# One function table for Ln and Exp, written table loads, and a chunk-by-chunk opening in a hybrid decoder layer

## The chip, the cores and the metric

The kernel runs on one core of one Trainium2 chip. The metric is the time of one execution on the device, in microseconds; of several runs the median is given. TensorE (PE in the rows), VectorE (DVE), ScalarE (ACT) and GpSimd (POOL) are the core's engines, SyncE (SP) issues most of the transfers.

## The reference, cut to what matters

One decoder layer over 512 tokens of width 1024, in float32:

```python
x = x + 0.5 * swiglu(rms_norm(x, ffn1_norm), ffn1_w_gate, ffn1_w_up, ffn1_w_down)
x = x + hybrid_mixer(rms_norm(x, mix_norm), ...)
x = x + 0.5 * swiglu(rms_norm(x, ffn2_norm), ffn2_w_gate, ffn2_w_up, ffn2_w_down)
return rms_norm(x, final_norm)
```

`swiglu` has a hidden width of 2816. `hybrid_mixer` projects once (`w_in`) and runs two branches on the result: a dilated sliding-window attention (12 heads of 64 in three groups, whose outputs are merged by their softmax denominators), and RWKV-7 time mixing (16 heads of 64):

```python
kk = kk / jnp.maximum(jnp.sqrt(jnp.sum(kk * kk, axis=-1, keepdims=True)), 1e-12)
# per token t and head: S_t = S_{t-1} diag(w_t) + (S_{t-1} a_t) b_t^T + v_t k_t^T ;  y_t = S_t r_t
g = jax.nn.sigmoid(zg) @ g2
yn = (y - mu) * lax.rsqrt(var + RWKV_GN_EPS)          # group norm of each head
merged = gates[:, :D] * y_attn + gates[:, D:] * y_rwkv # then one output projection
```

`zg` has 160 columns: 128 of them make one full projection of the kernel, the other 32 a small one.

## The kernel before, in words

**Layout and products.** Everything lies transposed: features on the 128 partitions, 512 tokens in the free dimension, so a matrix of activations is 8 chunks of 128x512. A float32 product is made of three matmuls in fp32r, `mm3` (L383): high part of the weight times high part of the activation (`xhi`), high times low (`xlo`), low times high. A weight of 128x1024 is 8 blocks, so 24 matmuls of 128x128 by 512 columns, called full matmuls here.

**Weights.** `wload` (L448) issues a weight's transfer on SyncE's queue into one of three raw buffers `wr`; `wsplit` (L459) copies it to `wh` on ScalarE and subtracts to `wl` on VectorE. There are two pairs of `wh` and `wl`, so the split of a weight waits for the last matmul of the one before the last. `wnext` and `wahead` call them, the latter after the third block of a weight.

**The start (from L501).** ScalarE loads the table that holds Sqrt. X comes in 8 chunks on SyncE's queue, the first weight in two halves between them; `vec`, the small vectors (the norm's gains among them), comes on GpSimd's queue. For each chunk `gain_chunk` makes `xhi` (ScalarE) and `xlo` (VectorE), and `sum_chunk` squares the chunk (ScalarE, `t` or `ssq`) and adds (VectorE). Then the feed-forward, `ffn`, goes weight by weight: the 24 matmuls of the first gate weight into one accumulator `facc`, the 24 of the first up weight into another, and after them `norm_rstd` (a matmul of the sum of squares by a constant, Sqrt, reciprocal). Since the scale 1/rms is applied behind the product, the matmuls needn't wait for it.

**The mixer.** Its calls are not issued as they are written but recorded as nodes of a `Plan`; `Plan.order` (L217) is a list scheduler that walks all engines with a cost for each node (`note`, from L131), a penalty for a change of the array's tile mode, and rules on buffers, and `emit` (L349) issues the nodes in that order. The projections are main work, in the order of the table `MAIN_ORDER`; beside them run streams of side work: `post` (for each of 8 head pairs: decay, norm of k, masks), `finish` (for four groups of two such pairs, called a pair here: inversion of the chunk's triangular matrices, then the recurrence over 8 chunks of 64 tokens with the state in `SVU`), `tail` (group norm, bonus and output gate of a pair) and `core` (two of attention). All matmuls of the side work are small, in float32.

**Tables.** Sigmoid and Tanh, Exp, Ln, Sqrt and Silu are table functions of ScalarE. The kernel before leaves the loads of the mixer to the compiler, which puts an `ACT_TABLE_LOAD` in front of a function whose table isn't the one loaded. `rsqrt` (L755), called in `post` and `tail` for each of the 8 head pairs, computes 1/sqrt as Exp(-0.5 Ln s) with a Newton step: Ln, Exp and Square on ScalarE, two operations on VectorE.

**The places of the change.** `rsqrt` and `tail` (L1123): the scale of the group norm's variance is a `tensor_scalar` on VectorE. `h_zg2` (L800) and the loop over `MAIN` (L1271): the small gate projection is `mm3` over 8 blocks of 32 columns, 24 matmuls. Lines 358 and 377 in the rows are helpers: L358 is the call in `emit`, so all that the plan issues, L377 the call of a `Queue` outside it, so both feed-forwards.

Of the kernel before, what the change touches and what calls it, by code (L numbers as in the profile page):

```python
# [17 lines left out]
P = 128  # L18
# [29 lines left out]
MAIN_ORDER = """  # L48
k.0 r.0 v.0 k.1 r.1 v.1 gate.0 gate.1 gate.2 gate.3 k.2 gate.4 r.2 v.2 r.3 k.3 v.3 gate.5 gate.6 gate.7 gate.8 k.4 r.4
v.4 k.5 r.5 gate.9 v.5 gate.10 gate.11 gate.12 gate.13 gate.14 gate.15 k.6 r.6 v.6 k.7 r.7 v.7 aq.0.0 av.0.0 aq.0.1  # L50
ak.0.1 av.0.1 aq.0.2 ak.0.0 av.0.2 ak.0.2 av.1.2 av.1.0 aq.1.0 aq.1.1 ak.1.0 ak.1.1 av.1.1 aq.1.2 ak.1.2 wout.0 wout.1
wout.2 wout.3 wout.4 wout.5 wout.6 aup.0 wout.7 aup.1"""
# [3 lines left out]
LAT, SLACK, WINDOW, HOLD, SETTLE = 0.07, 0.2, 40, 0.0, 3.5  # L56
URGENT, SIDE, MAIN_MM = range(3)


# [26 lines left out]
class Plan:  # L86


    TABLES = {"Sigmoid": "sigmoid", "Tanh": "sigmoid", "Exp": "exp", "Ln": "exp", "Sqrt": "sqrt", "Silu": "silu"}

    def __init__(self):
# [39 lines left out]
    def note(self, eng, op, call, outs, ins, func=None):  # L131
        tags = [k[0] for k in map(self.slot, outs + ins) if k]
        if eng == PE:
# [3 lines left out]
            c = n / 2400 + 0.0136 if x.dtype == F32R else 4 * n / 2400 + 0.01  # L137
            c = 0.018 if mode == (32, 32) else c * 0.5 if 64 in mode else c
            nd = self.open
# [77 lines left out]
    def order(self, keep):  # L217
# [19 lines left out]
        for nd in self.nodes:  # L237
            for tag in {k[0] for k in uses[nd]}:
                touch.setdefault(tag, []).append((nd, [k for k in nd.new if k[0] == tag], [k for k in uses[nd] if k[0] == tag and k in mortal]))

        def safe(nd):

            for tag in {k[0] for k in nd.new}:
                bufs = next(k[1] for k in nd.new if k[0] == tag)
                u = used.get(tag, 0) + sum(k[0] == tag for k in nd.new)
                if u > bufs:
                    return False
                rest = {}
                l = touch[tag] = [x for x in touch[tag] if x[0] not in done]
                for m, new, ends in l:  # L250
                    if m is not nd:
                        u += len(new)
                        if u > bufs:
                            return False
                    for k in ends:
                        n = rest[k] = rest.get(k, left[k]) - 1
                        if not n:
                            u -= 1
            return True

        while len(done) < len(self.nodes):
# [29 lines left out]
            elif eng == PE:  # L291
                if nd.mode[0] != mode:
                    c += 0.2 if nd.mode[0] == (128, 128) else 0.1
                mode = nd.mode[1]
                free[PE] = t + c
                end = t + c + 0.17
            else:
                if nd.table and nd.table != table:
                    c += 1.3
                    table = nd.table  # L300
                if nd.lock:
                    t = max(t, port)
                    port = t + c
                end = free[eng] = t + c
# [7 lines left out]
            for k in nd.new:  # L312
# [3 lines left out]
                self.place[k[2]] = f[1]  # L316
            for k in uses[nd]:
                left[k] -= 1
                if not left[k] and k in mortal:
# [29 lines left out]
    def emit(self, tc, keep):  # L349
        self.on = False  # L350
        with tc.manual_schedule():
            for nd in self.order(keep):
                for tag, _, name in nd.new:
                    if tag in self.rings:
# [37 lines left out]
def layer_kernel(ctx: ExitStack, tc, a, out):  # L392
# [110 lines left out]
    vec = const.tile([P, NVEC], F32, name="vec")  # L503
    G.dma_start(vec, a["vec"])
    cst = const.tile([P, CST["bd"]], F32, name="cst")
# [4 lines left out]
    A.preload_act_table_set("sqrt_and_others")  # L510
    xload(0)
    wload(2, lambda i: xload(1 + i))
    xload(3)
    wload()
    for m in range(4, DC):
        xload(m)
    Y.dma_start(cst, a["cst"][:, 0:CST["bd"]])
    wsplit(2)
    omka = const.tile([P, 8], F32, name="omka")
# [52 lines left out]
    def ffn(tag, X, hpool, tmp, rstd_fn, done, stack):  # L572
# [7 lines left out]
        for f in range(FC):  # L580
            pg, pu = facc(), facc()
            for part, ps in ((0, pg), (1, pu)):
                w = wnext((tag, "gu", f, part))
# [40 lines left out]
    def tmp():  # L624
        return hpool.tile([P, S], F32, tag="tmp", bufs=5, name=nm("t"))
    for m in range(DC):
        gain_chunk(X[:, m, :], col("ffn1_norm", m), m)
    wsplit()
    for m in range(DC):
        sum_chunk(ssq, X[:, m, :], m, tmp)  # L630
    ssq1 = acts.tile([P, S], F32, tag="ssqa", bufs=1, name=nm("ssq"))
# [60 lines left out]
def mixer(tc, a, env):  # L692
# [17 lines left out]
    with ExitStack() as st:  # L710
# [89 lines left out]
        def h_zg2(ps):  # L800
            z = shift_evac(ps, 2, 32)
            A.activation(z[0:32, 0:S], z[0:32, 0:S], AF.Sigmoid)
# [320 lines left out]
        def tail(q, Qt, YT, raws):  # L1123
            for hl in range(2):
# [7 lines left out]
                rs = b2()  # L1132
                V.tensor_scalar(rs[:, 0:S], ps, 1.0 / 64.0, GN_EPS, op0=ALU.mult, op1=ALU.add)
                rs = rsqrt(rs)
# [134 lines left out]
        rstd = None  # L1269
        wz = lora_w(lora_load(a["w_zg2"]))  # L1270
        for t in MAIN:  # L1271
            n = t[0]
            w = wnext(t)
            if n in handlers:
# [8 lines left out]
                if n == "zg":  # L1283
                    ps = acc()
                    plan.stream = "main"
                    for k in range(DC):
                        plan.cls = MAIN_MM
                        mm3(T, ps[0:32, :], wsl((wz[:, 0:256], wz[:, 256:512]), k, 32), xk(k), k == 0, k == DC - 1)
                        plan.cls = SIDE
# [157 lines left out]
```

## Time and profile before

| | |
|---|---|
| median of 3 runs | 1404.8 us (1403.41 to 1405.29) |
| the profiled execution | 1407.91 us, its span 1406.1 us |
| mean granted clock of TensorE | 0.99 |
| busy, of the span | TensorE 97%, VectorE 59%, ScalarE 43%, GpSimd 1% |
| transfers | 158.5 MB, mean 113 GB/s |

The stages by the timeline: first feed-forward to 374 us, projections with RWKV and then attention to 1032, with the output projections behind, second feed-forward and final norm to the end. A row of the trace's groups gives the operation, its output and inputs by name (`b` is any of the mixer's 128x512 work buffers, `ch`, `mi` and `acc` its PSUM tiles), the count, the busy time and the mean of one, and at the end the idle time of that engine just before these instructions and what ended it. A row of the timeline gives start, duration, engine, line, operation and count, and in brackets the idle time before it and its releaser.

### The profile page before, as it was taken

How to read it: one execution, taken by the hardware profiler on the slowest of the kernel's cores; microseconds unless marked ns; L12 is line 12 of the kernel's file. 1: busy time of each engine (PE TensorE's matmuls, PEld its weight loads, DVE VectorE, ACT ScalarE, POOL GpSimd, SP SyncE). 2: the span in 40 equal slices, each digit the busy share in tenths (PEclk: the TensorE clock that was granted, in tenths of full speed). 3: DMA queues.
4: the chain of work that ended last, by engine and by line, in shares of the span. 5: the costliest groups of instructions: out<-in, count | busy, mean ns of one | idle time of the engine just before them, and what ended most of it. 6: DMA issues, size and time to landing. Idle time of an engine off the chain costs nothing. (4 is left out here: it accounts for less than half of the span.)

```text
span 1406.1 us, 21794 instructions
## 1 busy us (share of the span) xinstructions
PE 1363.9 (97%) x8852; PEld 1099.1 (78%) x8852; DVE 832.2 (59%) x1299; ACT 598.9 (43%) x918; POOL 19.9 (1%) x75
## 2 busy tenths in 40 slices
PE   7999999999999999999999999899999999999997
PEld 5888888888777876776876777677888888888886
DVE  6444444333578786876987887666654444443324
ACT  5232332222484454554655444686443232322222
POOL 0000000000000000000000000000000000000000
PEclk9999999999999999999999999999999999999998
DMA  5232323343564432423522412343652323233333
GB/s 191 93 103 93 103 90 101 96 129 109 161 208 134 145 94 82 126 84 102 148 82 60 122 52 64 127 153 111 195 179 90 101 95 101 94 92 93 99 100 109
DMA packets 83732, 158.53 MB, mean 113 GB/s; under 512 B 32368, under 2 KB 37232, under 8 KB 83632
## 3 DMA queue, kind: packets, MB, share of 16 engines
q1 hardware_dynamic: 82384, 154.78, 35.3%
q10 hardware_dynamic: 1152, 2.10, 0.4%
q8 instruction: 69, 1.13, 0.3%
q0 software_dynamic: 96, 0.26, 0.1%
q14 instruction: 31, 0.25, 0.1%
HBM read 135.88 MB, written 20.45 MB: 111 GB/s over the span
## 5 line engine op out<-in xcount | busy, mean ns | idle before, releaser
L377 ACT ACTIVATE wh<-wr 128x1024 fp32r<-128x1024 f32 (+1 forms) x140 | 144.0, 1029 | 468.4 <-PE facc L377 257.7
L377 PE MATMUL facc<-xhi,wh 128*128 128x512 f32 x704 | 276.0, 392 | 7.1 <-ACT wh L377 7.1
L377 PE MATMUL facc<-xlo,wh 128*128 128x512 f32 x704 | 274.7, 390 | 0.0
L377 PE MATMUL facc<-xhi,wl 128*128 128x512 f32 x704 | 274.5, 390 | 0.2 <-DVE wl L377 0.2
L377 DVE TENSOR_TENSOR wl<-wr,wh 128x1024 fp32r<-128x1024 f32 (+1 forms) x140 | 165.5, 1183 | 142.4 <-ACT wh L377 142.4
L358 PE MATMUL acc<-xhi,wh 128*128 128x512 f32 x544 | 227.1, 417 | 0.0
L358 PE MATMUL acc<-xlo,wh 128*128 128x512 f32 x544 | 215.1, 395 | 1.1 <-issue 1.1
L358 PE MATMUL acc<-xhi,wl 128*128 128x512 f32 x544 | 215.2, 396 | 1.0 <-DVE wl L358 1.0
L377 DVE TENSOR_TENSOR t<-facc,rstd 128x512 f32<-128x512 f32 x88 | 60.6, 691 | 223.0 <-PE facc L377 223.0
L377 PEld LDWEIGHTS facc<-xhi,wh 128*128 128x128 f32 x704 | 132.5, 188 | 36.2 <-ACT wh L377 7.5
L377 PEld LDWEIGHTS facc<-xlo,wh 128*128 128x128 f32 x704 | 132.5, 188 | 29.0 <-DVE xlo L377 0.9
L377 PEld LDWEIGHTS facc<-xhi,wl 128*128 128x128 f32 x704 | 132.5, 188 | 28.2 <-DVE wl L377 1.1
L377 PE MATMUL facc<-hhi,wl 128*128 128x512 f32 (+1 forms) x374 | 141.0, 377 | 0.7 <-DVE wl L377 0.7
L377 PE MATMUL facc<-hhi,wh 128*128 128x512 f32 (+1 forms) x374 | 141.0, 377 | 0.0
L377 PE MATMUL facc<-hlo,wh 128*128 128x512 f32 (+1 forms) x374 | 140.9, 377 | 0.0
L358 DVE TENSOR_TENSOR b<-b,b 128x512 f32<-128x512 f32 (+6 forms) x187 | 112.0, 622 | 21.9 <-ACT b L358 13.0
L358 ACT ACTIVATE wh<-wr 128x1024 fp32r<-128x1024 f32 x78 | 82.5, 1057 | 97.7 <-PE acc L358 71.1
L358 PEld LDWEIGHTS acc<-xhi,wh 128*128 128x128 f32 x544 | 103.5, 190 | 25.4 <-issue 0.6
L358 PEld LDWEIGHTS acc<-xhi,wl 128*128 128x128 f32 x544 | 103.3, 190 | 24.6 <-DVE wl L358 1.8
L358 PEld LDWEIGHTS acc<-xlo,wh 128*128 128x128 f32 x544 | 103.6, 190 | 19.5 <-issue 1.7
L358 ACT ACTIVATE b<-b 128x512 f32<-128x512 f32 (+4 forms) x155 | 92.1, 604 | 28.0 <-DVE b L358 16.4
L358 DVE TENSOR_TENSOR wl<-wr,wh 128x1024 fp32r<-128x1024 f32 x78 | 95.0, 1219 | 12.0 <-ACT wh L358 11.5
(125 smaller groups left out, 1476.8 us busy)
## 6 DMA issues: line engine op xcount, KB each, us to landing
wr<-in_ffn_gu_dram SPq DMA_DIRECT2D x87, 512.0 KB
wr<-in_w_in_dram SPq DMA_DIRECT2D x60, 512.0 KB
wr<-in_ffn_down_dram SPq DMA_DIRECT2D x34, 512.0 KB
wr<-in_ffn_down_dram SPq DMA_DIRECT2D x17, 384.0 KB
gdr<-b SPq DMA_DIRECT2D x16, 256.0 KB
wr<-in_w_out_dram SPq DMA_DIRECT2D x8, 512.0 KB
b<-gdr SPq DMA_DIRECT2D x16, 256.0 KB
wr<-in_w_o_dram SPq DMA_DIRECT2D x8, 512.0 KB
```

The source lines that it names most:

```text
L358: f(*map(self.put, args), **{k: self.put(x) for k, x in kw.items()})
L377: return f(*args, **kw)
```

## The change

Six things, in the order of the diff. The table `MAIN_ORDER` is another, and the planner counts float32 matmuls, transposes and changes of the tile mode at other costs (a memo in its buffer rule, left out here, changes no decision). `emit` writes a table load itself whenever the table of the next node is not the last one it wrote, and names for Exp and Ln the one set that holds both. In the start, `vec` comes on ScalarE's queue, the first gate weight and the first up weight come in quarters of 256 columns between the chunks of X, and `opening` takes the place of the first pass of `ffn`: for each chunk the gain, on every second one the split of a quarter of both weights, then its three matmuls for gate and three for up; the split of the third weight and all squares follow after. In the group norm the scale goes to ScalarE. The small gate projection interleaves the high and the low columns of its weight, so that two matmuls of 72 columns take the place of three of 32, and `h_zg2` adds the two halves.

```diff
 WAHEAD = 2
 
 MAIN_ORDER = """
-k.0 r.0 v.0 k.1 r.1 v.1 gate.0 gate.1 gate.2 gate.3 k.2 gate.4 r.2 v.2 r.3 k.3 v.3 gate.5 gate.6 gate.7 gate.8 k.4 r.4
-v.4 k.5 r.5 gate.9 v.5 gate.10 gate.11 gate.12 gate.13 gate.14 gate.15 k.6 r.6 v.6 k.7 r.7 v.7 aq.0.0 av.0.0 aq.0.1
-ak.0.1 av.0.1 aq.0.2 ak.0.0 av.0.2 ak.0.2 av.1.2 av.1.0 aq.1.0 aq.1.1 ak.1.0 ak.1.1 av.1.1 aq.1.2 ak.1.2 wout.0 wout.1
+gate.0 k.0 r.0 v.0 k.1 r.1 v.1 gate.1 gate.2 gate.3 k.2 r.2 v.2 gate.4 r.3 k.3 v.3 gate.5 gate.6 gate.7 gate.8 gate.9
+gate.10 k.4 r.4 v.4 k.5 r.5 gate.11 v.5 gate.12 gate.13 gate.14 gate.15 k.6 r.6 v.6 k.7 r.7 v.7 aq.0.1 aq.0.0 ak.0.0
+av.0.0 ak.0.1 av.0.1 aq.0.2 ak.0.2 av.0.2 av.1.0 aq.1.1 aq.1.0 av.1.1 ak.1.1 aq.1.2 ak.1.0 ak.1.2 av.1.2 wout.0 wout.1
 wout.2 wout.3 wout.4 wout.5 wout.6 aup.0 wout.7 aup.1"""
...
     TABLES = {"Sigmoid": "sigmoid", "Tanh": "sigmoid", "Exp": "exp", "Ln": "exp", "Sqrt": "sqrt", "Silu": "silu"}
+    SETS = {"sigmoid": "sigmoid_and_others", "exp": "natural_log_exp_and_others", "sqrt": "sqrt_and_others"}
...
             n, k, m = x.free_size(), w.shape[0], w.free_size()
             mode = (32 if k <= 32 else 64 if k <= 64 else 128, 32 if m <= 32 else 64 if m <= 64 else 128)
             c = n / 2400 + 0.0136 if x.dtype == F32R else 4 * n / 2400 + 0.01
-            c = 0.018 if mode == (32, 32) else c * 0.5 if 64 in mode else c
+            if x.dtype != F32R:
+                c = 0.118 if op == "transpose" else max(n, m) / 600 + 0.01
+            c = 0.033 if mode == (32, 32) and not kw_pos(call) else 0.018 if mode == (32, 32) else c * 0.5 if 64 in mode else c
...
                 if nd.mode[0] != mode:
-                    c += 0.2 if nd.mode[0] == (128, 128) else 0.1
+                    c += 0.27 if nd.mode[0] == (128, 128) else 0.1
...
@@ -349,7 +365,11 @@
     def emit(self, tc, keep):
         self.on = False
         with tc.manual_schedule():
+            table = None
             for nd in self.order(keep):
+                if nd.table not in (None, table):
+                    table = nd.table
+                    tc.nc.scalar.preload_act_table_set(self.SETS[table])
...
     vec = const.tile([P, NVEC], F32, name="vec")
-    G.dma_start(vec, a["vec"])
+    A.dma_start(vec, a["vec"])
...
     A.preload_act_table_set("sqrt_and_others")
-    xload(0)
-    wload(2, lambda i: xload(1 + i))
-    xload(3)
+    first = [(wpool.tile([P, 1024], F32, tag="wraw", bufs=NRAW, name=nm("wr")), wpool.tile([P, 1024], F32R, tag="whi", bufs=NW, name=nm("wh")),
+              wpool.tile([P, 1024], F32R, tag="wlo", bufs=NW, name=nm("wl"))) for _ in range(2)]
+    pos[:] = 2, 2
+    for m in range(DC):
+        xload(m)
+        if m % 2 == 0:
+            c = slice(m * P, m * P + 2 * P)
+            for (raw, _, _), (_, ap, _) in zip(first, plan):
+                Y.dma_start(raw[:, c], ap[:, c])
+    Y.dma_start(cst, a["cst"][:, 0:CST["bd"]])
     wload()
-    for m in range(4, DC):
-        xload(m)
-    Y.dma_start(cst, a["cst"][:, 0:CST["bd"]])
-    wsplit(2)
...
             pg, pu = facc(), facc()
-            for part, ps in ((0, pg), (1, pu)):
+            if tag == "ffn1" and f == 0:
+                opening(pg, pu)
+                rstd = rstd_fn()
+            for part, ps in ((0, pg), (1, pu)) if tag == "ffn2" or f else ():
                 w = wnext((tag, "gu", f, part))
...
-    for m in range(DC):
-        gain_chunk(X[:, m, :], col("ffn1_norm", m), m)
-    wsplit()
-    for m in range(DC):
-        sum_chunk(ssq, X[:, m, :], m, tmp)
+
+    def opening(pg, pu):
+
+        with tc.manual_schedule():
+            for m in range(DC):
+                gain_chunk(X[:, m, :], col("ffn1_norm", m), m)
+                if m % 2 == 0:
+                    c = slice(m * P, m * P + 2 * P)
+                    for raw, hi, lo in first:
+                        split(raw[:, c], hi[:, c], lo[:, c])
+                for ps, w in zip((pg, pu), first):
+                    mm3(T, ps, wsl(w[1:], m), xk(m), m == 0, m == DC - 1)
+        wsplit()
+        for m in range(DC):
+            sum_chunk(ssq, X[:, m, :], m, tmp)
...
         def h_zg2(ps):
-            z = shift_evac(ps, 2, 32)
+            t = b2()
+            A.copy(t[0:32, 0:S], ps[32:64, :])
+            V.tensor_add(t[0:32, 0:S], ps[0:32, :], t[0:32, 0:S])
+            z = shift_evac(t[:, 0:S], 2, 32)
...
                 rs = b2()
-                V.tensor_scalar(rs[:, 0:S], ps, 1.0 / 64.0, GN_EPS, op0=ALU.mult, op1=ALU.add)
+                A.activation(rs[:, 0:S], ps, AF.Identity, bias=eps[:, 1:2], scale=1.0 / 64.0)
                 rs = rsqrt(rs)
...
-        wz = lora_w(lora_load(a["w_zg2"]))
+        wzr, wz = lora_load(a["w_zg2"]), b2(F32R)
+        wz3 = wz[:, 0:512].rearrange("p (k s m) -> p k s m", s=2, m=32)
+        wzr3 = wzr[:, 0:256].rearrange("p (k m) -> p k m", m=32)
+        A.activation(wz3[:, :, 0, :], wzr3, AF.Copy)
+        V.tensor_sub(wz3[:, :, 1, :], wzr3, wz3[:, :, 0, :].bitcast(F32))
+        G.memset(wz[:, 512:520].bitcast(F32), 0.0)
...
                     for k in range(DC):
                         plan.cls = MAIN_MM
-                        mm3(T, ps[0:32, :], wsl((wz[:, 0:256], wz[:, 256:512]), k, 32), xk(k), k == 0, k == DC - 1)
+                        for i, x_ in enumerate(xk(k)):
+                            T.matmul(ps[0:72, :], wz[:, 64 * k:64 * k + 72], x_, start=k + i == 0, stop=k + i == DC)
```

The places where the instructions of an engine stand otherwise:

ScalarE in the tail of the last RWKV pair, before (`b`, `ch` and `mi` are work buffers and PSUM tiles, `wh` a weight's high part):

```order
L358 COPY b_1270_8328<-ch_8300 128x512
L358 ACT_TABLE_LOAD
L358 ACTIVATE b_1164_8340<-b_1162_8335 128x512
L358 ACT_TABLE_LOAD
L358 ACTIVATE b_1163_8353<-b_1164_8340 128x512
L358 ACTIVATE b_1164_8340<-b_1163_8353 128x512
L358 ACT_TABLE_LOAD
L358 ACTIVATE b_1174_8359<-b_1172_8351 128x512
L358 ACT_TABLE_LOAD
L358 ACTIVATE b_1173_8367<-b_1174_8359 128x512
L358 ACTIVATE b_1174_8359<-b_1173_8367 128x512
L358 COPY b_1262_8277<-mi_8342 128x128
```

and now:

```order
L378 ACTIVATE wh_2741<-wr_2735 128x1024
L378 ACTIVATE b_1163_8386<-mi_8376,eps 128x512
L378 ACTIVATE b_1165_8393<-b_1163_8386 128x512
L378 ACTIVATE b_1164_8401<-b_1165_8393 128x512
L378 ACTIVATE b_1165_8393<-b_1164_8401 128x512
L378 ACTIVATE b_1173_8411<-mi_8396,eps 128x512
L378 ACTIVATE b_1175_8417<-b_1173_8411 128x512
L378 ACTIVATE b_1174_8425<-b_1175_8417 128x512
L378 ACTIVATE b_1175_8417<-b_1174_8425 128x512
L378 COPY b_1275_8436<-ch_8339 128x512
L378 ACTIVATE wh_2748<-wr_2739 128x1024
L378 ACTIVATE xhi<-b_1395_8357 128x512
```

The four table loads are gone, the two scales of the group norm (`b<-mi,eps`) have come in, and each half now runs scale, Ln, Exp, Square, with a weight's split on either side.

ScalarE at the end of the first feed-forward, before, where the last chunk of the mixer's input is split and squared (`X_74` is the residual, `rstd` the first norm of the mixer):

```order
L358 ACTIVATE wh_2474<-wr_2410 128x1024
L377 ACTIVATE xhi<-X_74,vec 128x512
L377 ACTIVATE t_2438<-X_74 128x512
L358 ACTIVATE rstd_2477<-acc_2476,eps 128x512
L358 ACTIVATE wh_2482<-wr_2472 128x1024
```

and now:

```order
L378 ACTIVATE wh_2492<-wr_2428 128x1024
L372 ACT_TABLE_LOAD
L397 ACTIVATE xhi<-X_74,vec 128x512
L397 ACTIVATE t_2456<-X_74 128x512
L378 ACTIVATE rstd_2495<-acc_2494,eps 128x512
```

A table load that `emit` writes stands between the second split of a mixer weight and the last chunk.

TensorE behind the 48 matmuls of the first gate and up weight, with the semaphores that an instruction waits for, before (`acc<-ssq,cst` is the matmul of the sum of squares, `facc` the accumulators):

```order
L377 MATMUL facc_165<-xlo,wh_129 128x512
L377 MATMUL facc_165<-xhi,wl_130 128x512
L377 MATMUL acc_222<-ssq_109,cst 128x512 [waits DMAHW3_49,DVE_49]
L377 MATMUL facc_236<-xhi,wh_203 128x512 [waits Activation_49]
L377 MATMUL facc_236<-xlo,wh_203 128x512
```

and now:

```order
L397 MATMUL facc_128<-xhi,wl_84 128x512
L397 MATMUL facc_252<-xhi,wh_212 128x512 [waits Activation_49]
L397 MATMUL facc_252<-xlo,wh_212 128x512
L397 MATMUL facc_253<-xhi,wh_267 128x512 [waits Activation_49]
L397 MATMUL facc_253<-xlo,wh_267 128x512
L397 MATMUL facc_252<-xhi,wl_213 128x512 [waits DVE_49]
L397 MATMUL facc_252<-xhi,wh_212 128x512
L397 MATMUL facc_252<-xlo,wh_212 128x512
L397 MATMUL acc_238<-ssq_114,cst 128x512 [waits DMAHW1_49,DVE_49]
```

The matmul of the sum of squares has gone back behind matmuls of the third and the fourth weight (`wh_212`, `wh_267`). On ScalarE the split of the third, `wh_212`, now stands behind six squares (`t`), and the fourth's behind one more:

```order
L397 ACTIVATE xhi<-X_74,vec 128x512
L397 ACTIVATE t_217<-X_74 128x512
L397 ACTIVATE t_220<-X_74 128x512
L397 ACTIVATE t_223<-X_74 128x512
L397 ACTIVATE t_226<-X_74 128x512
L397 ACTIVATE t_229<-X_74 128x512
L397 ACTIVATE t_232<-X_74 128x512
L397 ACTIVATE wh_212<-wr_102 128x1024
L397 ACTIVATE t_235<-X_74 128x512
L397 ACTIVATE wh_267<-wr_254 128x1024
```

## Rows read from the trace of the kernel before

**Rows 1.** The page: busy time by engine, and the transfer rate in 40 slices.
```profile
PE 1363.9 (97%) x8852; PEld 1099.1 (78%) x8852; DVE 832.2 (59%) x1299; ACT 598.9 (43%) x918; POOL 19.9 (1%) x75
...
GB/s 191 93 103 93 103 90 101 96 129 109 161 208 134 145 94 82 126 84 102 148 82 60 122 52 64 127 153 111 195 179 90 101 95 101 94 92 93 99 100 109
```
**Rows 2.** Windows: length, busy time of PE, PEld, DVE, ACT, POOL, PEclk, DMA share, GB/s.
```profile
22.00:373.00 351.00, 351.00 (x1549) 290.47 (x1548) 153.85 (x178) 106.68 (x130) 0.00 (x0) 1.00 0.33 103
520.00:900.00 380.00, 361.04 (x3829) 276.82 (x3827) 295.63 (x566) 206.50 (x384) 14.05 (x39) 0.98 0.32 95
900.00:1032.00 132.00, 127.88 (x646) 103.87 (x643) 86.39 (x144) 78.71 (x130) 0.00 (x0) 0.97 0.46 151
```
**Rows 3.** Groups by line, ScalarE: count, busy time, mean ns, idle time before.
```profile
L358 ACT ACT_TABLE_LOAD x46 | 59.0, 1283 | 4.0 <-DVE dc L358 1.4 <-DMA b<-gdr 1.2 <-DVE b L358 0.4
...
L377 ACT ACT_TABLE_LOAD x6 | 7.7, 1283 | 0.8 <-PEq L1436 0.7
```
**Rows 4.** Timeline, ScalarE in the last pair's tail, VectorE in the third's.
```profile
883.80 1.28 ACT L358 ACT_TABLE_LOAD   x1 [0.44 <-DVE b L358]
885.10 0.63 ACT L358 ACTIVATE b<-b 128x512 f32<-128x512 f32 x1
...
887.04 1.29 ACT L358 ACTIVATE b<-b 128x512 f32<-128x512 f32 x2
...
708.88 1.42 DVE L358 SCALAR_TENSOR_TENSOR b<-b,b 128x512 f32<-128x512 f32 x2 [2.53 <-ACT b L358]
```
**Rows 5.** Timeline, waits of TensorE in the mixer.
```profile
530.11 0.69 PE L358 MATMUL ch<-b,b 128*64 128x64 f32 x16 [1.49 <-DVE b L358]
...
591.22 0.33 PE L358 MATMUL ch<-b,b 64*64 64x64 f32 x4 [1.81 <-DVE b L358]
...
634.55 0.53 PE L358 MATMUL ch<-b,b 128*64 128x64 f32 x6 [1.07 <-ACT b L358]
...
712.52 1.69 PE L358 MATMUL ch<-b,b 32*32 32x32 f32 x128 [1.50 <-issue]
...
744.09 0.69 PE L358 MATMUL ch<-b,b 128*64 128x64 f32 x16 [0.95 <-DVE b L358]
...
784.45 0.66 PE L358 MATMUL mi<-cst,b 128*128 128x128 f32 x4 [0.68 <-DVE b L358]
...
893.38 1.97 PE L358 MATMUL ch<-cst,b 128*128 128x128 f32 x8 [5.47 <-ACT b L358]
...
970.81 1.52 PE L358 MATMUL acc<-b,wh 128*128 128x512 f32 x2 [2.03 <-ACT b L358]
```
**Rows 6.** Windows behind two of these waits (columns as in rows 2).
```profile
713.00:719.00 6.00, 6.00 (x138) 4.98 (x137) 5.86 (x10) 0.72 (x1) 0.00 (x0) 0.72 0.27 90
893.00:900.00 7.00, 6.62 (x47) 5.77 (x47) 4.62 (x7) 4.30 (x10) 0.00 (x0) 0.57 0.40 147
```
**Rows 7.** Timeline, TensorE: first matmul of the small gate projection, first behind it.
```profile
383.73 0.40 PE L358 MATMUL acc<-xhi,b 128*32 128x512 f32 x1
...
389.32 0.40 PE L358 MATMUL acc<-xhi,wh 128*128 128x512 f32 x1
```
**Rows 8.** Timeline, the opening: ScalarE, then TensorE.
```profile
5.25 0.72 ACT L377 ACTIVATE xhi<-X,vec 128x512 fp32r<-128x512 f32 x1 [3.23 <-DMA vec<-in_vec_dram]
...
6.39 0.61 ACT L377 ACTIVATE wh<-wr 128x512 fp32r<-128x512 f32 x1
...
17.22 1.06 ACT L377 ACTIVATE wh<-wr 128x1024 fp32r<-128x1024 f32 x1
...
7.06 0.79 PE L377 MATMUL facc<-xhi,wh 128*128 128x512 f32 x1 [7.06 <-ACT wh L377]
...
21.58 1.02 PE L377 MATMUL acc<-ssq,cst 128*128 128x512 f32 x2
```
**Rows 9.** Timeline, the seam into the mixer: VectorE, then TensorE.
```profile
373.49 0.69 DVE L377 TENSOR_TENSOR ssq<-ssq,t 128x512 f32<-128x512 f32 x1
...
374.70 1.02 PE L358 MATMUL acc<-ssq,cst 128*128 128x512 f32 x2
```

More of the change, by code (lines that the diff above doesn't have):

```diff
@@ L57, with kw_pos @@
 URGENT, SIDE, MAIN_MM = range(3)
+def kw_pos(call):
+    return "tile_position" in call[2]
 class Node:
@@ L239, in order, with find @@
                 touch.setdefault(tag, []).append((nd, [k for k in nd.new if k[0] == tag], [k for k in uses[nd] if k[0] == tag and k in mortal]))
+        known, moved = {}, dict.fromkeys(touch, 0)
         def safe(nd):
+            at = [moved[k[0]] for k in nd.new]
+            if known.get(nd, (0, 0))[0] != at:
+                known[nd] = at, find(nd)
+            return known[nd][1]
+        def find(nd):
             for tag in {k[0] for k in nd.new}:
@@ L317, in order @@
             for k in uses[nd]:
+                moved[k[0]] += 1
                 left[k] -= 1
```

## Prediction

> **What bounds the kernel now.** The page comes first: TensorE is busy for 1363.9 of 1406.1 us, VectorE for 832.2, ScalarE for 598.9 [rows 1]. So TensorE is the bound, and a change can gain only in three ways: fewer or shorter matmuls, less of the 42 us in which TensorE stands still, or a higher granted clock in the stretches after a stand-still. The busy time in windows says where the stand-still lies. In the gate and up part of the first feed-forward it is nil, 351.00 of 351.00 us; in the second half of the RWKV work it is 380 - 361.0 = 19.0 us, and in the attention 132 - 127.9 = 4.1 us [rows 2]. The rest is the start, 7.06 us before the first matmul, and the end of the kernel.
>
> Then the groups by line, for ScalarE: 46 + 6 loads of a function table at 1283 ns each, 66.7 us of ScalarE [rows 3]. That time costs nothing as long as TensorE has other work. The timeline of ScalarE in the tail of the last RWKV head pair shows the pattern: Ln, load, Exp and Square, load, Ln, load, Exp and Square. Nothing but the load stands between them: the activation behind the load of 883.80 starts at 885.10. VectorE waits for such a chain for 2.53 us at 708.88 [rows 4]. The timeline of TensorE says where a wait for such a chain reaches it. I looked at each wait of TensorE over 0.6 us in the mixer, and went to ScalarE and VectorE ahead of it. Six of them end with something that stood behind one or two loads: 1.49, 1.07, 1.50 (put down to "issue", but its operand comes from VectorE, late from the wait at 708.88 [rows 4]), 0.95, 0.68 and 5.47 us, in all 11.2. Two of the same size have no load ahead of them, 1.81 at 591 and 2.03 at 970.81 [rows 5]. Last, the granted clock: it is 0.72 in the six microseconds after the wait at 712 and 0.57 in the seven after the wait at 893, between the levels 0.5 (1.2 GHz) and 1.0 (2.4 GHz); the gate and up part, which never waits, has 1.00 [rows 2, 6].
>
> **The change part by part,** against the profiled execution's 1407.9 us (span 1406.1, and 1.8 around it).
>
> *One table for Ln and Exp.* The changed program loads 18 tables where it loaded 52; the loads between Ln and Exp are gone, those for Sigmoid, Sqrt and Silu stay. 34 x 1.283 = 43.6 us less of ScalarE, of which nothing counts but the six waits, 11.2 us [rows 5]. Where a chain loses one or two loads, 1.3 to 2.6 us, a wait of 1.5 or less is gone. The wait of 5.47 needs more: in the old order everything of the last tail is alone with ScalarE's eight steps and four loads. Now the eight steps remain, at 0.63 to 0.65 each [rows 4], 5.2 us, and in the new order two of the weight splits and 27 full matmuls (9, 6 and 12, 0.233 each, so 6.3 us) lie beside them. That covers it but for 0 to 2.0 us; I take 1.0 as still waited. **-10.2** (bounds -9.2 and -11.2).
>
> *The clock behind two of these waits.* What the lower clock cost is (1 - 0.72) x 6 = 1.7 us and (1 - 0.57) x 7 = 3.0 us [rows 6]. In both places the clock was whole until TensorE had stood for 1.5 us or more. Without the stand, **-4.7** (0 if a new wait of that length stands there).
>
> *The second gate projection in 16 matmuls for 24.* Its 24 matmuls run from 383.73 to 389.32, 0.233 each, though they fill 32 columns of the array only [rows 7]; 16 with 72 columns have the same 512 rows to stream. 8 x 0.233, **-1.9**. The added copy on ScalarE and addition on VectorE lie in a part where the matmuls of the next weights cover them.
>
> *The opening.* Before, the first matmul starts at 7.06, behind the split of half a weight on ScalarE (0.61 from 6.39), which stands behind the first xhi (0.72 from 5.25) and its square; the 48th ends its slot at 21.58, so 14.5 us for 48 x 0.233 = 11.2 [rows 8]. Now the squares come later and the split is of a quarter, 0.40 by the rows for a half and a whole (0.61 and 1.06): start 5.25 + 0.72 + 0.40 = 6.4. The 48th then ends between 6.4 + 11.2 = 17.6 and 21.6; I take 19.3, since the transfers of X and of two weights, 3 MB, all have to be there (191 GB/s in the page's first slice of forty makes 15.7 us from the first issue [rows 1]). That is 2.3 gained. Then comes the new cost. The split of the third weight needs the buffer that the 45th matmul frees, and now stands on ScalarE behind six squares (of the shape of the 0.63 in [rows 4], so 3.8 us); a further square and the fourth weight's split (1.06) stand ahead of TensorE's fourth matmul from there, where it had no such wait before. I count 1.06 + 0.63 plus 0.1 of start as stand, 1.8 us. **-0.5** (bounds -2.2 and +3.0: the low one if the squares fit into the wait for the buffer, the high one if the 48th ends at 21.6 and 1.2 us of squares come after the wait as well).
>
> *The seam into the mixer.* The program now writes out each table load, and its first one, Sqrt, is of a table that is loaded already; it stands between a weight's split and the last chunk's xhi and square. Before, the sum of squares is ready at 373.49 + 0.69 = 374.18, and TensorE asks for it at 374.70 [rows 9]. With 1.283 more [rows 3] it is ready at 375.46: **+0.8** (0 to +1.3). The Trainium skill ("ScalarE: Activation LUTs", section "What ACT_TABLE_LOAD costs") puts some 1.38 us of drained pipeline beside the load, about 2.7 us per switch; the trace shows none of it, 1.30 us from the start of the load to the next activation [rows 4], and by the page this term would be about +2.1 for +0.8.
>
> *The end of the attention.* The wait of 2.03 at 970.81 is for ScalarE's split of the attention's output [rows 5]; in the new order six full matmuls stand between the last product with V and the first use of that split. 6 x 0.233, **-1.4** (0 to -2.0).
>
> *Group norm's scale on ScalarE.* Eight steps of 0.68 go from VectorE to ScalarE. VectorE has 296 of 380 us busy, ScalarE 207 [rows 2], and ScalarE loses more by the loads than it takes: 0.
>
> *The new order.* The mixer's main matmuls and its side work are dealt anew by other prices. The third pair's recurrence has stretches with few full matmuls beside it in this order, and each of its hand-overs (TensorE to VectorE or ScalarE and back) can show. No row prices it; the nearest are the waits of 0.68 and 0.95 [rows 5], and three of those at the smaller price make **+2.0** (bounds -3, if it rather hides the 1.81 at 591 and its like, and +8, if eight or so show with 0.95 each).
>
> Sum: -10.2 - 4.7 - 1.9 - 0.5 + 0.8 - 1.4 + 2.0 = -15.9, so 1407.9 - 15.9 = 1392.0 for an execution like the profiled one. That one was 3.1 over the median of the runs, 1404.8; the prediction for a median is 1392.0 - 3.1 = **1389**.
>
> **The rivals.** *More.* The new order also hides the wait at 591 (1.81) and takes the 2.0 of the sum with it, and the opening reaches its low bound, 1.7 more: 1389 - 1.8 - 2.0 - 1.7 = 1383. For it: 19 us of stand in the second half of the recurrence leave much to win [rows 2]. Against: three things have to meet. 0.12.
>
> *The opening late.* The first weights come as quarters of 128 KB in turn with X on one queue; if each pair of chunks waits for its quarter, the 48th matmul ends at 21.6 or later and the 1.8 of stand come on top: +2.3 and up to 2 more than the sum, 1389 + 3 to 5 = 1392 to 1394. The Trainium skill ("DMA: Bandwidth & Descriptors", section "Bandwidth") advises batching transfers to 1 MiB and more, which speaks against quarters, and no row of the kernel before has a quarter. 0.12.
>
> *Other waits take the place.* A table load is the last thing that a wait ended with, not all that was late: the chains also wait for the sum over a head on TensorE and for VectorE's own queue. If half of the 10.2 comes back as a later releaser and one of the two clock falls stays, -15.9 + 5.1 + 3.0 = -7.8: 1397; if nearly all does, -2 to -3: 1402. For it: the waits of 1.81 and 2.03, which no load causes [rows 5]. Against: the wait of 5.47, half of the gain, has four loads and nothing else in it [rows 4]. 0.20, of which 0.06 within 0.2% of no change.
>
> *Slower.* The recurrence is 4 head pairs of 8 chunks, 32 steps, and each hands over from TensorE to VectorE and ScalarE and back. The old order keeps full matmuls of the main work beside nearly all; rows of 1.49 and 1.07 show what one uncovered step costs [rows 5]. If the new order, with gates and projections drawn forward, leaves the late steps bare, at 0.55 us a step on average it costs 32 x 0.55 = 17.6, more than the whole gain, and with a clock fall of 3.0 [rows 6] on top the time is 1404.8 - 17.9 + 17.6 + 3.0 = 1407.5, where 17.9 is the sum without its +2.0. It decides from some 0.5 us a step. Against: the count of main matmuls is the same, and the old order with worse chains loses 19 us in 380 for everything. 0.05.
>
> **How the numbers follow.** My forecast, 1385 to 1392, has 0.51; the rivals 0.12, 0.12, 0.20 and 0.05. The range takes the first case and most of the second, the late opening, and the third to 1399: **1381 to 1399**, with 0.1 left out above and some below. What a measurement can tell from no change is 0.2%, 2.8 us. Faster by more: 0.51 + 0.12 + 0.12 + 0.14 = **0.89**; within it **0.06**; slower **0.05**.
>
> **What would show it.** In the trace after: 18 table loads; in the last pair's tail no load between Ln and Exp, the wait at 893 at most 2 us and a granted clock near 1 behind it; 16 matmuls in 3.7 us for the second gate projection; a first matmul at 6.4 and a stand of 1 to 3 us some 13 us after it; a wait of 0.5 to 1.3 us for the sum of squares at the seam. The prediction is wrong if the loads go and TensorE's stand in the second half of the recurrence stays above 15 us, or if the granted clock there is no higher than 0.98.

## The result, and the profile after

The changed kernel takes 1382.97 us (median of 4 runs, 1381.36 to 1384.9) against 1405.05 us (4 runs): the ratio is 0.9844, with an interval of 0.9826 to 0.9862, so 22 us faster. The profiled execution took 1381.36 us, the fastest of the four, and the profiled one of before 1407.91, so between the two profiles there are 26.5 us; the forecast for the profiled one was 1392.0.

The page of the changed kernel, busy time by engine [rows 1]:

```profile
PE 1350.9 (98%) x8844; PEld 1093.6 (79%) x8844; DVE 827.3 (60%) x1297; ACT 561.9 (41%) x898; POOL 19.8 (1%) x75
```

TensorE is 13.0 us less busy with 8 matmuls fewer, and stands still for 28.7 us (1379.6 - 1350.9) where it was 42.2. Where that lies shows in the windows from the mixer's sum of squares to the first matmul of the second feed-forward, of the kernel before and of the changed one (length, PE, PEld, DVE, ACT, POOL, granted clock, DMA share, GB/s):

```profile
374.70:1031.51 656.81, 631.34 (x5573) 492.83 (x5572) 500.99 (x899) 369.84 (x636) 18.44 (x68) 0.98 0.39 119
```

```profile
376.73:1005.98 629.25, 617.38 (x5564) 486.10 (x5565) 495.31 (x892) 330.54 (x610) 19.46 (x69) 1.00 0.40 124
```

All of the gain is in the mixer: 656.81 - 629.25 = 27.6 us, of which 13.6 is stand-still (25.5 before, 11.9 now) and 14.0 busy time, at a clock of 1.00 for 0.98. In these two traces the start lost 2.0 (376.73 for 374.70), and the end, 374.6 and 373.6 us, gained 1.0.

The groups of ScalarE have 18 loads [rows 3]:

```profile
L372 ACT ACT_TABLE_LOAD x12 | 15.4, 1283 | 0.2
...
L397 ACT ACT_TABLE_LOAD x6 | 7.7, 1283 | 1.3 <-PEq L1481 1.2
```

The tail of the last pair, timeline of ScalarE [rows 4]: scale, then Ln, Exp and Square in one run of 1.96, twice:

```profile
872.87 0.67 ACT L378 ACTIVATE b<-mi,eps 128x512 f32<-128x512 f32 x1
873.57 1.96 ACT L378 ACTIVATE b<-b 128x512 f32<-128x512 f32 x3
875.44 0.67 ACT L378 ACTIVATE b<-mi,eps 128x512 f32<-128x512 f32 x1
876.14 1.96 ACT L378 ACTIVATE b<-b 128x512 f32<-128x512 f32 x3
```

The waits of TensorE over 0.6 us that are left in the mixer are 7 [rows 5], the longest of them:

```profile
602.62 0.33 PE L378 MATMUL ch<-b,b 32*32 32x32 f32 x17 [2.06 <-issue]
...
710.66 0.21 PE L378 MATMUL ch<-b,b 32*32 32x32 f32 x1 [2.30 <-issue]
...
742.90 0.69 PE L378 MATMUL ch<-b,b 128*64 128x64 f32 x16 [1.34 <-DVE b L378]
...
888.73 0.66 PE L378 MATMUL mi<-cst,b 128*128 128x128 f32 x4 [1.78 <-DVE b L378]
```

The 5.47 of the last tail is gone. In the window of [rows 2] TensorE now stands still for 380 - 370.27 = 9.7 us, at a clock of 1.00, so neither of the prediction's signs of being wrong (above 15 us, 0.98 or less) appeared:

```profile
520.00:900.00 380.00, 370.27 (x3964) 286.11 (x3964) 302.29 (x581) 184.85 (x379) 14.10 (x39) 1.00 0.34 103
```

The opening on TensorE [rows 8], and the seam [rows 9]:

```profile
5.19 0.80 PE L397 MATMUL facc<-xhi,wh 128*128 128x512 f32 x1 [5.19 <-ACT wh L397]
...
7.54 0.63 PE L397 MATMUL facc<-xhi,wl 128*128 128x512 f32 x1
9.25 0.80 PE L397 MATMUL facc<-xhi,wh 128*128 128x512 f32 x1 [1.08 <-ACT xhi L397]
...
14.04 0.63 PE L397 MATMUL facc<-xlo,wh 128*128 128x512 f32 x1
...
23.51 0.50 PE L397 MATMUL facc<-xhi,wh 128*128 128x512 f32 x1 [0.73 <-ACT wh L397]
...
24.77 1.02 PE L397 MATMUL acc<-ssq,cst 128*128 128x512 f32 x2
...
376.73 1.13 PE L378 MATMUL acc<-ssq,cst 128*128 128x512 f32 x2 [0.27 <-DVE ssq L397]
```

The first matmul is 1.9 us earlier, at 5.19. Then TensorE waits 1.08 for the second chunk of X, and its matmuls stand 0.43 us apart until 14.5, for 0.23 afterwards. The small gate projection runs from 385.90 to 389.58 [rows 7].

### The profile page after: what moved, and what is told of

Same layout as the page of the kernel before. It is cut to its first block, busy times and chain, and to the rows that moved or that the text cites. A ratio compares the mean times of both kernels' runs of the same rounds, so it can differ in the third digit from the quotient of the medians.

```text
span 1379.6 us, 21787 instructions
## 1 busy us (share of the span) xinstructions
PE 1350.9 (98%) x8844; PEld 1093.6 (79%) x8844; DVE 827.3 (60%) x1297; ACT 561.9 (41%) x898; POOL 19.8 (1%) x75
## 4 chain that ended last, share of the span: by engine, by line
PE 92%; DVE 4%; ACT 2%; issue 1%; DMA 1%; SPq 0%; DVEq 0%; ACTq 0%
PE facc L397 52%; PE acc L378 29%; PE ch L378 6%; PE mi L378 5%; DVE b L378 2%; ACT b L378 1%; DVE wl L378 0%; ACT L372 0%; DVE X L397 0%; DMA X<-in_x_dram 0%; PE acc L397 0%; ACT wh L378 0%; DMA wr<-in_w_out_dram 0%; DVE xlo L378 0%; ACT xhi L397 0%
## 5 line engine op out<-in xcount | busy, mean ns | idle before, releaser
L397 ACT ACTIVATE wh<-wr 128x1024 fp32r<-128x1024 f32 (+2 forms) x145 | 144.7, 1000 | 463.5 <-PE facc L397 254.3
L397 DVE TENSOR_TENSOR wl<-wr,wh 128x1024 fp32r<-128x1024 f32 (+2 forms) x145 | 166.1, 1147 | 140.0 <-ACT wh L397 138.2
```

The source lines that it names most:

```text
L397: return f(*args, **kw)
```

## The experiments

The theory: the gain comes from the loads, by the waits that end behind them and the clock that falls behind those waits. The rivals: the new order of the mixer brings it, and the loads were hidden; or, for the size of it, the opening. All ratios are to the kernel before, run on the same chip.

**The loads alone, in both orders.** The first takes the written loads out of the changed kernel, the second puts them into the kernel before. Neither moves anything else on any engine.

```diff
-                if nd.table not in (None, table):
-                    table = nd.table
-                    tc.nc.scalar.preload_act_table_set(self.SETS[table])
```

> The changed kernel without the loads that the program writes: the compiler puts them in again, Exp and Ln in separate tables, 50 loads for 18; order of the mixer, opening and small projection stay the changed ones. If the gain comes from the loads (my forecast: 10 us of waits and 5 of clock), 10 to 16 us come back: 1393 to 1399. If the new order brought the gain and the loads are hidden, under 3 us: 1383 to 1386.

Measured: 1409.88 us, ratio 1.0035 (1.0022 to 1.0049). That is 27 us above the changed kernel, and 5 above the kernel before.

```diff
+    SETS = {"sigmoid": "sigmoid_and_others", "exp": "natural_log_exp_and_others", "sqrt": "sqrt_and_others"}
...
+                if nd.table not in (None, table):
+                    table = nd.table
+                    tc.nc.scalar.preload_act_table_set(self.SETS[table])
```

> The kernel before with one thing changed: the program writes the loads, one table for Exp and Ln, 20 loads for 52; order, opening and small projection of before. If the loads bring the gain: 1405 - 15 = 1390, within 1388 to 1394, with the wait of 5.47 at 893 down to 0 to 2. If the new order brings it: 1400 or more, since what was behind a load then waits for something else.

Measured: 1385.14 us, ratio 0.9856 (0.9844 to 0.9869). So 32 loads fewer bring 20 us by themselves, in the old order, and in the new one 27. The loads are nearly all of the gain, and more than I had priced. The mixer's window of this second kernel; its waits over 0.6 us in the mixer, all but one of 0.86; and the two places where the kernel before waited 1.81 (584.11 here) and 5.47 (871.84):

```profile
374.67:1009.75 635.08, 624.35 (x5572) 489.92 (x5573) 500.93 (x899) 327.25 (x603) 18.90 (x68) 0.99 0.40 123
```

```profile
584.11 0.33 PE L363 MATMUL ch<-b,b 64*64 64x64 f32 x4 [0.49 <-DVE b L363]
...
595.22 1.35 PE L363 MATMUL ch<-b,b 32*32 32x32 f32 x124 [0.90 <-issue]
...
598.77 0.50 PE L363 MATMUL acc<-xlo,wh 128*128 128x512 f32 x1 [1.07 <-issue]
...
871.84 1.10 PE L363 MATMUL ch<-cst,b 128*128 128x128 f32 x8 [0.23 <-ACT b L363]
...
874.27 0.66 PE L363 MATMUL mi<-cst,b 128*128 128x128 f32 x4 [0.63 <-DVE b L363]
...
924.62 3.16 PE L363 MATMUL ch<-own,b 128*128 128x16 f32 x16 [1.77 <-ACT b L363]
...
949.11 1.52 PE L363 MATMUL acc<-b,wh 128*128 128x512 f32 x2 [2.03 <-ACT b L363]
```

Against the kernel before, in the same order: 14.7 us less stand-still (25.5 to 10.7) and 7.0 less busy time for the same matmuls (631.34 to 624.35). Of the six waits that I had put down to loads, 11.2 us in all, 0.23 is left (with a new one of 0.63 just behind it); 2.03, in the attention, stayed as expected, and so did the 1.77 beside it. But the 1.81 at 591, which I had counted as not of the loads, is down to 0.49 as well. It hung on them from further off: in the kernel before VectorE waited 2.11 us at 567.25 behind loads, some 20 us upstream:

```profile
562.07 1.28 ACT L358 ACT_TABLE_LOAD   x1
563.98 0.63 ACT L358 ACTIVATE b<-b 128x512 f32<-128x512 f32 x1 [0.63 <-DVE b L358]
564.63 1.28 ACT L358 ACT_TABLE_LOAD   x1
565.92 1.30 ACT L358 ACTIVATE b<-b 128x512 f32<-128x512 f32 x2
567.24 1.28 ACT L358 ACT_TABLE_LOAD   x1
...
567.25 1.42 DVE L358 SCALAR_TENSOR_TENSOR b<-b,b 128x512 f32<-128x512 f32 x2 [2.11 <-ACT b L358]
```

That loads are what the wait at 591 hung on is shown by the pair: it is the same order, instruction for instruction, with 32 loads fewer. That it was the loads of this place, and which of them, is not.

**The order.** Table of main work and prices of before in the changed kernel; then the old table alone, then the old prices alone.

```diff
-gate.0 k.0 r.0 v.0 ...
+k.0 r.0 v.0 k.1 ...
-                c = 0.118 if op == "transpose" else max(n, m) / 600 + 0.01
...
-                    c += 0.27 if nd.mode[0] == (128, 128) else 0.1
+                    c += 0.2 if nd.mode[0] == (128, 128) else 0.1
```

> The changed kernel with the table of main work and the prices of before; loads, opening, small projection and group norm as changed. By the forecast the order was worth +2.0 - 1.4, about nothing: 1382 to 1385. If the order brings the gain: 1394 to 1402, and TensorE's stand-still in the mixer goes from 12 us towards 25.

Measured: 1387.84 us (1383.99 to 1392.95), ratio 0.9873 (0.9852 to 0.9894): by the medians some 4 us slower than the changed kernel, between the two expectations. Its runs spread over 9 us, and the intervals of the two ratios overlap, so this difference is likely but not firm. TensorE's stand-still in the mixer is 14.5 us for 11.9.

> The changed kernel with the old table of main work, but the new prices of the planner. With table and prices both old it was 1387.8 against 1383.0. If the table is what brings the difference: 1386 to 1389; if the prices do: 1382 to 1385.

Measured: 1398.25 us, ratio 0.9949 (0.9937 to 0.9961): 15 us slower than the changed kernel, slower than either expectation. A single wait, for VectorE, is 6 us:

```profile
593.96 0.48 PE L378 MATMUL ch<-b,b 64*64 64x64 f32 x4 [6.19 <-DVE b L378]
```

> The changed kernel with the prices of the planner before, and the new table of main work. If table and prices only work as a pair (old table with new prices gave 1398): 1388 or more. If the table carries the gain by itself: 1382 to 1385.

Measured: 1420.66 us, ratio 1.0115 (1.0096 to 1.0134): slower than the kernel before, though the loads are gone. Long waits for ScalarE and VectorE stand in this order, the longest where the RWKV branch's outcome goes into the output projection:

```profile
840.77 0.48 PE L376 MATMUL ch<-b,b 64*64 64x64 f32 x4 [4.98 <-DVE b L376]
...
938.07 0.80 PE L376 MATMUL acc<-xhi,wh 128*128 128x512 f32 x1 [10.15 <-ACT xhi L376]
```

Neither half of the order's change is worth anything alone: table and prices belong together, and a mismatched pair costs 15 or 38 us.

**The group norm's scale.**

```diff
-                A.activation(rs[:, 0:S], ps, AF.Identity, bias=eps[:, 1:2], scale=1.0 / 64.0)
+                V.tensor_scalar(rs[:, 0:S], ps, 1.0 / 64.0, GN_EPS, op0=ALU.mult, op1=ALU.add)
```

> The changed kernel with the group norm's scale on VectorE, as before. Forecast 0: 1381 to 1385, with ScalarE 5 us less busy and VectorE 5 us more. If ScalarE is the engine whose chain ends the tails, 1 to 3 us faster; if VectorE is, 1 to 3 us slower.

Measured: 1394.58 us, ratio 0.9926 (0.9911 to 0.9941), 12 us slower. It would be wrong to read this as the price of eight operations on VectorE: their engine is part of the plan, so the planner dealt the mixer anew, and of the instructions of VectorE and TensorE hundreds stand elsewhere. The stand-still in the mixer is 15.2 us and the clock 0.98. What the scale's engine costs in an unchanged order stays open.

**The opening.** Four kernels with the changed mixer, its order untouched, and the changed one once more. First the opening of before:

```diff
-    A.dma_start(vec, a["vec"])
+    G.dma_start(vec, a["vec"])
...
-            if tag == "ffn1" and f == 0:
-                opening(pg, pu)
+    wsplit(2)
```

> The changed kernel with the opening of before (weight by weight, halves, squares in between, vec on GpSimd's queue). By the trace of the changed kernel the sum of squares of the mixer is 2.0 us later than before, 1.1 of it by the eighth matmul of the second pair of weights: without the new opening 1 to 2 us faster, 1381 to 1382, and the first weights' 56 matmuls done by about 24.1 for 25.2. If the later seam is only the spread between executions and the opening gains 0.5 as forecast: 1383.5.

Measured: 1379.76 us (1376.73 to 1380.79), ratio 0.9813 (0.9798 to 0.9828): by the medians about 3 us faster than the changed kernel, though the intervals of the two ratios still touch (0.9826 to 0.9862 there). The mixer's sum of squares is 2.3 us earlier than in the changed kernel's trace (376.73):

```profile
374.44 1.13 PE L378 MATMUL acc<-ssq,cst 128*128 128x512 f32 x2 [0.27 <-DVE ssq L397]
```

The changed kernel once more:

> The changed kernel once more beside the others, for a tighter interval and to see whether its first matmuls wait for the second chunk of X as before (1.08 us, then half rate until 14.8). If that wait is at the brink, it is shorter in some executions, and the runs spread over 2 us or more; median 1382 to 1384.

Measured: 1381.86 us (1380.36 to 1384.67), ratio 0.9835 (0.9819 to 0.985). The wait for the second chunk of X was 0.68 this time, for 1.08, and the matmul of the first sum of squares at 24.03, for 24.77. The old opening's 1379.76 is 2 us under this median, and the two intervals overlap.

Then without the redundant load at the seam:

```diff
-            table = None
+            table = "sqrt"
```

> The changed kernel without the first written load (Sqrt, of a table that is loaded already). Forecast: 0.8 at the seam; the trace showed a wait of 0.27 us there: 0.2 to 0.3 us faster than the changed kernel, not to be told from it in the time, and no wait for the sum of squares at the seam.

Measured: 1379.37 us (1378.32 to 1385.97), ratio 0.9826 (0.9807 to 0.9844), more below the changed kernel than the 0.2 to 0.3 expected, but with runs 7.6 us apart. The seam's wait of 0.27 is gone. In this execution the second chunk of X came in time, with no wait over 0.6 in the first 15 us, and the first sum of squares was at 21.97, with the program of the opening the same as in the changed kernel:

```profile
5.21 0.80 PE L397 MATMUL facc<-xhi,wh 128*128 128x512 f32 x1 [5.21 <-ACT wh L397]
...
20.35 0.50 PE L397 MATMUL facc<-xhi,wh 128*128 128x512 f32 x1 [0.73 <-ACT wh L397]
...
21.97 1.02 PE L397 MATMUL acc<-ssq,cst 128*128 128x512 f32 x2
```

One program, and 2.8 us between 21.97 and 24.77: what differs is when X lands, and how long TensorE then stays at the slower spacing. So one trace of each doesn't price the opening. All traces do it better, by the start of the mixer's sum of squares at the seam: in the three kernels with the old opening it is at 374.4 to 374.7, in the eight with the new one (the loads', the order's and the group norm's experiments have the same) at 373.5 to 376.7, with a median of 375.8. By these the new opening gains nothing and costs about 1 us, within a spread of 3; that is not all of the 2 to 3 us between the medians of the times, and the kernel without the load, with the new opening, is as fast as the one with the old. The other way to start early, the old opening with `vec` on ScalarE's queue (and no redundant load):

```diff
-    G.dma_start(vec, a["vec"])
+    A.dma_start(vec, a["vec"])
```

> The changed kernel with the opening of before, but vec on ScalarE's queue, and without the first written load (Sqrt, loaded already): the version that the first four runs point to. With the old opening alone the median was 1379.8. vec came at 5.0 there and X at 4.1 in the new opening, so the first matmul starts up to 0.9 earlier, at 5.9 to 6.2; the seam waits 0.27 less: 1378.5 to 1379.5. Rival: the earlier first matmuls only run at half rate longer, and the transfers of X still set the 48th: 1379.8, no gain.

Measured: 1379.27 us (1378.39 to 1379.96), ratio 0.9815 (0.9802 to 0.9828): the same as with the old opening alone. The first matmul came at 6.04 for 6.82, but then TensorE waited 0.69 for X, and the sum of squares came at 22.14, later than the 20.89 there. The rival was right: an earlier first matmul bought nothing. Last, two chunks of X ahead of each pair of quarters:

```diff
-        if m % 2 == 0:
-            c = slice(m * P, m * P + 2 * P)
+        if m % 2 == 1:
+            c = slice(m * P - P, m * P + P)
```

> The changed kernel without the extra load, and with two chunks of X ahead of each pair of weight quarters instead of one. If the changed opening loses time by TensorE's wait for the second chunk of X and the half rate after it, then here, with the first matmul at 5.7 to 6.2, there is no wait over 0.3 us in the first 15 us, the sum of squares is at 21.5 to 22.2 and the median is 1377 to 1379.5 with a spread under 3 us. If only the start counts, all is 0.8 later: 1380 to 1382.

Measured: 1379.9 us (1376.11 to 1381.05), ratio 0.9817 (0.98 to 0.9835). There was no wait over 0.3 us in the first 15, as expected; but the sum of squares was at 22.98, since matmuls behind the 48th still waited 0.24 and 0.59 for splits, and the spread was 4.9 us. So the wait for X is not all that the new opening loses: both pairs of weight buffers come free only at its end, and the third and the fourth split have nothing to hide behind. Even so the mixer's sum of squares, at 373.15, is the earliest of all these traces: with X in time, the chunk-by-chunk opening is no loss in this execution. The kernels with the old opening, with X first, or without the extra load lie at 1379.3 to 1379.9, and the runs don't tell them apart; each median lies 2 to 4 us under those of the changed kernel.

## Why the prediction was right, and where its sizes were off

The direction, the mechanism and the range held: 1383 against a forecast of 1389 within 1381 to 1399. The 22 us are 1.4 times the forecast's 16. Between the two profiles it is 26.5 (the one of before lies 2.9 over its kernel's median, the one after 1.6 under): the pair's mixer makes 21.7 of it (loads and clock), the rest of the change in the mixer 5.8 and the end 1.0, and the start takes back 2.0. So the sum was too low by 6.8 at loads and clock, by 4.5 at the order and its end of the attention, and by 1.0 at the end, and 1.7 the other way at the start: the last is an error that happened to bring the sum nearer. The time is that of the rival *More* (1383), but not by its way: the order did gain instead of costing 2.0, but the wait at 591 went with the loads, and the opening did not reach its low bound. Term by term:

- **One table for Ln and Exp, -10.2.** Right for what it priced: the six waits, matched matmul by matmul in the same order, gave 10.9, within the bounds. But the pair in the old order gives 14.7 us of stand-still. The step that failed is the list of waits. "Two of the same size have no load ahead of them" sorted one of the two wrongly: I looked for a load directly ahead of what TensorE waited for, and the 1.81 at 591 came from loads further upstream (1.3 us). And the list was not "each wait over 0.6 us in the mixer": there are 14 of them, I sorted eight. Of the other six, two went with the loads (1.2 us; to 0 and 0.22), the others stayed within 0.2 us. The last 1.3 us are the balance of shorter waits and of two that grew (0.90 at 595.22 and 0.63 at 874.27). The two that went, in the kernel before:

```profile
430.23 0.49 PE L358 MATMUL acc<-xhi,wl 128*128 128x512 f32 x1 [0.63 <-DVE wl L358]
...
501.01 0.69 PE L358 MATMUL ch<-b,b 32*32 32x32 f32 x56 [0.76 <-issue]
```

- **The clock, -4.7.** My two places were right, but not all: in the kernel before the granted clock was 0.50 (1.2 GHz) in stretches of together 20.5 us of the mixer, at the waits of 591, 712, 893, 948 and 971; in the pair's second kernel in 10.2 us, at the two waits of the attention. At half rate that is 5.1 us gained. The busy time of the same matmuls fell by 7.0; the rest is not accounted for. In the changed kernel one fall is left, behind the wait of 2.30 at 710.66.
- **The second gate projection, -1.9.** 389.58 - 385.90 = 3.7 for 5.6: as said.
- **The opening, -0.5 (bounds -2.2 and +3.0).** Wrong in sign, within the bounds: some +1 by the traces' seams (+2.0 in the profiled execution, seam included). The early start was better than forecast (5.19 for 6.4), and the waits for the third and fourth split were there (0.24 and 0.73, for 1.8), but the step "the 48th then ends between ... and 21.6; I take 19.3" took the full rate of 0.233 for granted. Early matmuls ran at 0.43 each, and the wait of 1.08 for X was followed by another five microseconds at that rate, so that the 48th ended at 21.6. My rival of a late opening had the quarters late; it was X that was, queued behind them. (The 3 MB of that step are 3.15 in the units of the rate, 16.5 us and not 15.7.)
- **The seam, +0.8.** It waited 0.27 in the changed kernel and in the pair's second kernel. The load itself takes what the row says: in the rows of the kernel before shown above, the load of 564.63 starts where the activation ahead of it ends (563.98 + 0.63), and the next activation starts at 565.92, 1.29 later, as in [rows 4]. The Trainium skill ("ScalarE: Activation LUTs", section "What ACT_TABLE_LOAD costs") puts about 1.38 us of drain beside the load of every switch to a different set; with that figure the seam, as an estimate, would have been about 2 us. These rows, whose loads are such switches, show no drain.
- **The end of the attention, -1.4, and the new order, +2.0.** Together +0.6 in the forecast. With the loads alone 635.08 us, with all of the change 629.25: -5.8 for the order, the group norm and the small projection, and -3.9 without the 1.9 of the last. So order and group norm together were a small gain, which the order's experiment above (some 4 us) fits. The wait of 2.03 went, and new ones came: 2.06 and 2.30 at "issue", 1.78 before the attention. The rival "slower by the new order" is not what happened, but its mechanism is real: a mismatched pair of table and prices costs 15 or 38 us.
- **The group norm, 0.** Not tested in an unchanged order.

With two tables for Ln and Exp, as in the kernel before, the rest of the change makes it 5 us slower (1409.88). Without the one table the sign would have been that of the slower rival.

## What to carry to other kernels

A load of a function table counts by the chains that hang on ScalarE, not by its share of ScalarE's time: sort a wait of the bound engine to a cause only after following its chain back through two or three engines, or better by a kernel that is the same order without the loads. Where a planner deals the work, an edit to one cost or one engine deals all of it anew; a part of the change can be priced only where the order is the same on both sides. And an earlier first matmul was worth nothing by itself: what counted was that the data for the second and third group were there when the first was done. Where executions of one program differ by as much as the effect, as in the opening, one trace of each side doesn't price it.

## What the runs showed of the hardware that I had not expected

The first matmuls of an execution ran 0.43 us apart, for 0.23 later. In the changed kernel the slow spacing lasted from 5.19 to 14.5 with a wait of 1.08 in it; in the kernel with two tables, whose opening is the same and whose wait was 0.25, matmuls stood 0.23 apart from 9.5 on. The windows of the changed kernel give a clock of 1.00 in both stretches:

```profile
10.00:12.00 2.00, 2.00 (x6) 1.58 (x6) 2.00 (x5) 2.00 (x5) 0.00 (x0) 1.00 1.07 326
...
16.00:20.00 4.00, 4.00 (x19) 3.34 (x18) 3.67 (x7) 3.11 (x6) 0.00 (x0) 1.00 0.92 302
```

But that 1.00 is no granted clock: the trace has no record of the clock before 14.70 us, and a window counts time without a record as 1.00. The first record, of 1.00, begins at 14.70, where the spacing falls; in the kernel with two tables it begins at 8.02, in the one without the extra load at 8.60. Where the mixer of the kernel before has a record of 0.50 (1.2 GHz), equal matmuls take the same 0.63 and stand the same 0.43 apart:

```profile
951.00:953.00 2.00, 2.00 (x7) 1.54 (x6) 1.26 (x3) 1.06 (x1) 0.00 (x0) 0.50 0.44 169
```

```profile
952.08 0.63 PE L358 MATMUL acc<-xhi,wh 128*128 128x512 f32 x1
952.50 0.63 PE L358 MATMUL acc<-xlo,wh 128*128 128x512 f32 x1
```

So the first matmuls ran as at the lower level, and the window's clock doesn't show it; the spacing of equal matmuls does.

The waits of 2.06 and 2.30 that the trace puts down to "issue" lie, by the count of the rows (111 and 17, 127 and 1), inside a group of 128 records of small matmuls (32x32), of which only the first few have a semaphore to wait for. The second of them is there in the trace of every kernel with this order, 2.1 to 2.7 us long; the first is 0.5 to 2.1 us in six of seven. Their cause stays open.
